# A hybrid decoder layer on one core: the gate and up projections as seven block products, with weight sums kept in DRAM

## The chip, the core and the metric

The kernel runs on one core of a Trainium2 chip. The metric is the device time of one execution in microseconds, as the median of several runs. Before the change it is 3034.36 us (three runs, 3031.14 to 3038.17).

## What is computed

One layer of a decoder for 2048 prompt tokens and 64 sample tokens (8 sequences of 8), together T = 2112. The first part (norm, a combined input projection, dilated window attention and a gated linear attention) is the same in both kernels. The change touches what follows:

```python
x1 = x + rmsnorm(concat(A, B) @ w_o, g_post)
h  = rmsnorm(x1, g_pre2)
gate = causal_dwconv3(h @ W_g)          # depthwise, 3 taps per channel
y  = x1 + rmsnorm((gelu(gate) * (h @ W_u)) @ W_down, g_post2)
```

The model width is 1024 (8 blocks of 128, KT), the hidden width 2816 (22 tiles of 128, NF). Everything is float32. The convolution's last two gate columns of every hidden channel are outputs too.

## The kernel before

Every product of matrices is made of three matmuls. `split` (L63 to L69) takes a float32 tile apart into a high part in a shorter format (`hi`, made by ScalarE, L66) and the rest (`lo` = source - `hi`, by GpSimd or VectorE, L69); `gemm` (L86 to L100) issues `wh·xh`, `wh·xl` and `wl·xh` for each block of the contraction and accumulates them in PSUM. `weight` (L73 to L84) loads a raw weight tile through SyncE's queue (L77) and splits it.

The span has three stages. Up to 1235 us run the first part's projections and the attention; this stage is not touched. Then comes `tail`, in two stages: the output projection (1235 to 1467 us) and the feed-forward part (1467 to 3011 us, with an end of 30 us behind it).

Tokens lie in the columns. The tail works in three chunks of 704 tokens (FCH: two halves of 352, 352 and 352, 448 and 256); a matmul works on one half.

- Output projection, `wo`, for each chunk: 8 output tiles (`pbo`), each of 8 blocks x 3 x 2 halves = 48 matmuls; the tile's weight (512 KB) is loaded and split anew in each chunk. VectorE copies the result out of PSUM (L61), ScalarE squares it (L1177) and the squares are added up (`bssq`, L1178) for the norm.
- `post`, for each chunk: a norm over the channels. Its matmuls `pn` (L125) sum the squares over the partitions; then come the gain (L1285), the addition of the residual (L1287), a second sum of squares, a second norm, and x1 and the factors of the second norm are stored in DRAM. It is a generator; its steps are interleaved with the next chunk's output tiles, and the last chunk's with the feed-forward part. `pb` (L136) spreads the factors over the partitions.
- `ffn_x`, for each chunk: x1 times the gain and the factor (L1309), then a split: the moving operand of the feed-forward part.
- `ffn`, for each chunk: hidden tiles in groups of 4, 4, 4, 4, 3 and 3 (FG). For each tile, a gate product (`pfg`, 48 matmuls, own weight of 512 KB), copies out of PSUM (L1339, L1340), two convolution taps on VectorE (L1349) with small copies of the two edge columns (`halo`, L1336 and L1347), the Gelu (L1355), an up product (`pfu`, 48 matmuls, another weight of 512 KB), the product of both (L1360) and its split (`hh`, `hl`). After a group, the down projection of its tiles (`pfd`) into 8 output tiles, added to an accumulator (L1390). All weights are loaded and split anew for each of the three chunks.
- `ffn_end` does the last group of the last chunk in two halves, and `final` makes the last norm, the residual (L1450 on VectorE, L1457 on GpSimd) and the store.

Tiles live in rings of buffers. The order of instructions on each engine is set by a scheduler of the framework, which goes by the order in the program, by its own model of durations and by when buffers come free; a dependency between two matmuls can pin their order. PSUM is used as four slots of two banks each.

Of the kernel before, what the change touches and what calls it, by code (L numbers as in the profile page):

```python
# [1 line left out]

# [24 lines left out]
FCH = ((0, 352, 352), (704, 352, 352), (1408, 448, 256))  # L27
FG = (4, 4, 4, 4, 3, 3)
# [6 lines left out]
class Layer:  # L35
# [35 lines left out]
    wc = None  # L71

    def weight(self, src, shape, lo_eng="p"):  # L73
        nc, p = self.nc, self.wpool
        pr, b = (self.xpool, self.wb[1] // 2) if self.wc is not None else (p, self.wb[1])
        raw = pr.tile(shape, F32, name=self.n("wr"), tag="wr", bufs=self.wb[0])
        nc.sync.dma_start(raw, src)  # L77
        if self.wc is not None:
            p = self.xpool if self.wc % self.wb[1] < b else p
            self.wc += 1  # L80
        hi = p.tile(shape, F32R, name=self.n("wh"), tag="wh", bufs=b)
        lo = p.tile(shape, F32R, name=self.n("wl"), tag="wl", bufs=b)
        self.split(hi, lo, raw, lo_eng)
        return hi, lo  # L84
# [30 lines left out]
    def rms_bcast(self, ssq, w, out, pool, psum, tag, shape=(128, 512), bufs=None, gap=2, lead=0, eng="a"):  # L115
# [8 lines left out]
        for j in range(nb):  # L124
            self.pnmm = nc.tensor.matmul(ps[:n, j:j + 1], ssq[:, o[j]:o[j] + n], self.ones, start=True, stop=True)  # L125
            self.gate("n", self.pnmm)
# [1029 lines left out]
    def subt(self, ps, c):  # L1156
        _, n0, n1 = FCH[c]
        return [(ps[:, 0, :n0], 0, n0), (ps[:, 1, :n1], n0, n1)]

    def t768(self, name, tag, bufs, dt=F32):  # L1160
        return self.npool.tile([128, self.W], dt, name=self.n(name), tag=tag, bufs=bufs)

    def hl(self, dt=F32R):
        p, b = (self.xpool, self.xb) if self.hc % 12 < self.xb // 2 else (self.npool, self.hlb - self.xb)
        self.hc += 1
        return tuple(p.tile([128, self.W], dt, name=self.n(n), tag="hl", bufs=b) for n in ("xh", "xl"))

    def raw(self):
        return self.xpool.tile([128, self.W], F32, name=self.n("br"), tag="raw", bufs=self.SB["xr"])

    def ssq_add(self, ssq, src, w, first, eng="p"):
# [3 lines left out]
        else:  # L1175
            sq = self.t768("sq", "sq", 2)
# [13 lines left out]

    def tail(self):
        tc, nc, a = self.tc, self.nc, self.a
        with ExitStack() as ctx:
            self.xpool = self.pool(ctx, "tx", side="right")
            self.gk = "h"
            self.W, self.hlb, self.wb = max(n0 + n1 for _, n0, n1 in FCH), self.SB["thl"], (2, 4)
            self.bx = [self.xpool.tile([128, self.W], F32, name=self.n("bx"), tag="px", bufs=3) for _ in range(3)]
            if self.SB["tw"]:
                self.wpool = self.pool(ctx, "tw")
            p = self.npool = self.pool(ctx, "tn")  # L1200
            if not self.SB["tw"]:
                self.wpool = self.pool(ctx, "tw")
            self.hc, self.xb = 0, self.SB["xb"]
            self.wc = 0 if self.SB["wx"] else None
            self.psum = self.pool(ctx, "tps", bass.MemoryType.PSUM)
            self.W, self.hlb, self.wb = max(n0 + n1 for _, n0, n1 in FCH), self.SB["thl"], (2, 4)
            pend = None
            for _ in self.wo_x(0):
                pass
            for c in range(3):  # L1210
                nxt = self.wo_x(c + 1) if c < 2 else self.ffn_x(0)
                for m, _ in enumerate(self.wo(c, self.xnext)):
                    if m >= 4:
                        next(nxt, None)
                    if pend is not None:
                        next(pend, None)
                        next(pend, None)
                for _ in nxt:
                    pass
# [476 lines left out]
```

## Time and profile before

| what | value |
|---|---|
| median of three runs | 3034.36 us |
| the profiled execution's own time | 3042.51 us |
| its span | 3040.7 us, mean granted TensorE clock 0.965 |
| first part | 0 to 1235 us |
| output projection | 1235 to 1467 us |
| feed-forward part | 1467 to 3011 us |
| last norm, residual, store | 3011 to 3041 us |
| bytes moved by the DMA | 378.92 MB, on average 125 GB/s |
| loads of gate and up weights | 132 of 512 KB |

The profile is one execution recorded by the hardware. Engines are PE (TensorE's matmuls), PEld (its weight loads), DVE (VectorE), ACT (ScalarE), POOL (GpSimd) and SP (SyncE, which here only issues transfers). A row of the groups of instructions has the line of the kernel, the engine, the operation, out<-in by the program's names with shapes and the count, then the busy time in us and the mean of one in ns, then the idle time of the engine right before them and what ended it. A row of the windows has, for a stretch of the span in us, its length, each engine's busy time with the number of instructions, the granted TensorE clock (1.00 is full), the share of time in which the DMA engines were busy and the GB/s they moved. A row of the waits has who waited for whom: us in total, times, the longest. A row of the timeline or of the chain has a start, a duration and the instruction; for a DMA the duration goes from issue to landing. Matmuls are pipelined, so what a matmul costs is the time from one start to the next and not its recorded duration.

### The profile page before, as it was taken

To read this page: it belongs to the slowest core of one execution; us is meant where nothing else is said; L and a number is where in the kernel's file an instruction comes from. 1 tells how busy PE (TensorE), PEld (TensorE's weight loads), DVE (VectorE), ACT (ScalarE), POOL (GpSimd) and SP (SyncE) were. 2 spreads that over 40 slices of the span, in tenths; PEclk is the share of its full clock that TensorE was granted. 3 is DMA by queue.
4 is the path that set the end of the run, shared out by engine and by line. 5 is a ranking of instruction groups with operands and counts; after the bars stand their busy time and mean duration, and the time that the engine had idled before them with its cause. 6 is when DMAs were issued, how large, how long until landed. Compare 5 with 4: busy or idle time off the path is not lost.

```text
span 3040.7 us, 50534 instructions
## 1 busy us (share of the span) xinstructions
PE 2870.4 (94%) x19738; PEld 2656.2 (87%) x19738; DVE 1382.0 (45%) x3263; ACT 1174.8 (39%) x2529; POOL 1426.2 (47%) x1014
## 2 busy tenths in 40 slices
PE   7988999999979999899899999999999999999996
PEld 5777788888767777798899999999999999999996
DVE  7686865344346655467732222371222236222225
ACT  5445444233256656333442232333222243322222
POOL 5656553334324465655443433574433366343343
PEclk9999999999989979999899999999999999999998
DMA  5323325699786665455432212252222224222222
GB/s 172 112 88 113 112 70 190 209 343 367 261 166 133 143 143 120 138 170 173 149 107 74 63 56 62 91 163 80 75 68 62 64 90 125 66 77 77 69 60 84
DMA packets 192975, 378.92 MB, mean 125 GB/s; under 512 B 19520, under 2 KB 91616, under 8 KB 187616
## 3 DMA queue, kind: packets, MB, share of 16 engines
q1 hardware_dynamic: 187680, 346.45, 36.2%
q0 software_dynamic: 5056, 29.24, 4.3%
q8 instruction: 155, 2.54, 0.4%
q14 instruction: 84, 0.69, 0.1%
HBM read 320.68 MB, written 54.94 MB: 124 GB/s over the span
## 4 chain that ended last, share of the span: by engine, by line
PE 51%; DVE 5%; ACT 1%; issue 1%; DMA 1%; POOL 0%; SPq 0%; ACTq 0%; DVEq 0%
PE pfd L94 16%; PE pfg L94 16%; PE pfu L94 15%; PE pbo L94 3%; DVE acc L1450 1%; DVE bssq L1178 1%; DVE bmo L1285 1%; DVE ct L1349 1%; DVE bmo L1287 0%; PE pn L125 0%; DMA br<-d_mixb 0%; ACT sq L1177 0%; DVE xl L69 0%; DVE br L1309 0%; DVE bmo L61 0%
## 5 line engine op out<-in xcount | busy, mean ns | idle before, releaser
L69 POOL TENSOR_TENSOR wl<-wr,wh 128x1024 fp32r<-128x1024 f32 (+2 forms) x386 | 780.2, 2025 | 1047.2 <-ACT wh L66 984.7
L66 ACT ACTIVATE wh<-wr 128x1024 fp32r<-128x1024 f32 (+2 forms) x389 | 347.7, 895 | 893.6 <-PE pfg L94 303.0
L1347 DVE COPY halo<-gt 128x2 f32<-128x2 f32 x66 | 48.8, 740 | 561.9 <-ACT gt L1339 561.9
L94 PE MATMUL pfu<-xh,wl 128*128 128x352 f32 (+2 forms) x1056 | 255.8, 323 | 0.0
L94 PE MATMUL pfg<-xh,wh 128*128 128x352 f32 (+2 forms) x1056 | 255.8, 323 | 0.0
L94 PE MATMUL pfu<-xh,wh 128*128 128x352 f32 (+2 forms) x1056 | 255.8, 323 | 0.0
L94 PE MATMUL pfu<-xl,wh 128*128 128x352 f32 (+2 forms) x1056 | 255.7, 323 | 0.0
L94 PE MATMUL pfg<-xh,wl 128*128 128x352 f32 (+2 forms) x1056 | 255.6, 323 | 0.0
L94 PE MATMUL pfg<-xl,wh 128*128 128x352 f32 (+2 forms) x1056 | 255.5, 323 | 0.0
L366 PE MATMUL pv<-wh,xh 128*128 128x256 f32 (+1 forms) x816 | 238.2, 292 | 9.0 <-DVE th L657 4.5
L94 PE MATMUL pfd<-hl,wh 128*128 128x352 f32 (+1 forms) x1008 | 243.3, 324 | 1.5 <-POOL hl L69 1.5
L94 PE MATMUL pfd<-hh,wh 128*128 128x352 f32 (+1 forms) x1008 | 240.1, 325 | 3.6 <-ACT hh L66 3.6
L94 PE MATMUL pfd<-hh,wl 128*128 128x352 f32 (+1 forms) x1008 | 242.9, 324 | 0.0
L366 PE MATMUL pv<-wl,xh 128*128 128x256 f32 (+1 forms) x816 | 235.2, 288 | 0.0
L366 PE MATMUL pv<-wh,xl 128*128 128x256 f32 (+1 forms) x816 | 234.8, 288 | 0.0
L1390 DVE TENSOR_TENSOR acc<-acc,pfd 128x352 f32<-128x352 f32 (+1 forms) x224 | 105.0, 517 | 282.3 <-PE pfd L94 282.3
L1511 ACT ACTIVATE ass<-ass,aml 128x256 f32<-128x256 f32 (+1 forms) x384 | 174.5, 456 | 122.3 <-DVE aml L1506 120.4
L94 PE MATMUL pq<-xh,wh 128*128 128x512 f32 (+2 forms) x480 | 173.3, 368 | 11.1 <-ACT xh L223 8.1
L94 PEld LDWEIGHTS pfu<-xh,wl 128*128 128x128 f32 x1056 | 176.8, 188 | 2.6
L94 PEld LDWEIGHTS pfg<-xh,wl 128*128 128x128 f32 x1056 | 176.8, 188 | 2.5
L94 PEld LDWEIGHTS pfg<-xh,wh 128*128 128x128 f32 x1056 | 176.7, 188 | 2.5
L94 PEld LDWEIGHTS pfg<-xl,wh 128*128 128x128 f32 x1056 | 176.6, 188 | 2.5
(316 smaller groups left out, 6540.0 us busy)
## 6 DMA issues: line engine op xcount, KB each, us to landing
wr<-in_wu SPq DMA_DIRECT2D x132, 512.0 KB
wr<-in_wt SPq DMA_DIRECT2D x95, 512.0 KB
wr<-in_wd SPq DMA_DIRECT2D x96, 256.0 KB
skp<-in_ckt SPq DMA_DIRECT2D x16, 1024.0 KB
svp<-in_cv SPq DMA_DIRECT2D x16, 1024.0 KB
av<-out_o_vp SPq DMA_DIRECT2D x192, 64.0 KB
wr<-in_wo SPq DMA_DIRECT2D x24, 512.0 KB
raw<-in_xn SPq DMA_DIRECT2D x40, 256.0 KB
```

Source lines behind the costliest of these rows:

```text
L66: nc.scalar.activation(hi, src, AF.Copy)
L69: (nc.gpsimd if lo_eng == "p" else nc.vector).tensor_tensor(lo, src, hi.bitcast(F32), op=ALU.subtract)
L94: mm = nc.tensor.matmul(o, ww[:, k, :], xx[:, s0:s0 + n], start=(k == order[0] and i == 0), stop=(k == order[-1] and i == 2))
L366: mm = nc.tensor.matmul(ps[:m, :256], x[:, t0:t0 + m], w[:, k % 4, :], start=(k == 0 and i == 0), stop=(k == KT - 1 and i == 2))
L1178: return (nc.gpsimd if eng == "p" else nc.vector).tensor_tensor(ssq[:, :w], ssq[:, :w], sq[:, :w], op=ALU.add)
L1285: nc.vector.scalar_tensor_tensor(o[:, :w], o[:, :w], self.gv[:, 1, m:m + 1], rb[:, :w], op0=ALU.mult, op1=ALU.mult)
L1347: nc.vector.tensor_copy(halo[:, f, :], gt[:, npr:npr + 2])
L1349: nc.vector.scalar_tensor_tensor(ct[:, :npr], gt[:, tap:tap + npr], self.cw[:, f, tap:tap + 1], ct[:, :npr], op0=ALU.mult, op1=ALU.add)
L1390: nc.vector.tensor_tensor(acc[m][:, s0:s0 + n], acc[m][:, s0:s0 + n], pz, op=ALU.add)
L1450: st = e1.scalar_tensor_tensor(am, am, self.gv[:, 3, m:m + 1], rb[:, :w], op0=ALU.mult, op1=ALU.mult)
L1511: nc.scalar.activation(ssb[:, sc:sc + nk], ssb[:, sc:sc + nk], AF.Exp, bias=self.ml[:, idx, h:h + 1], scale=-1.0, accum_out=self.ml[:, idx ...
```

## The change

**Chunks.** Four chunks of 528 tokens (two halves of 264), hidden groups of 2, 4, 4, 4, 4, 4 tiles. All buffers of the tail have 528 columns. PSUM is used as eight single banks.

**Gate and up projection.** `strassen` replaces `gemm` there. It takes two hidden tiles together as a block matrix: two halves of the contraction (4 blocks each) by two tiles, times two halves of the contraction by two halves of the tokens. In place of eight block products there are seven, of 4 blocks x 3 matmuls x 264 columns, so 84 matmuls a call where the plain way has 96; a call is made for each pair of tiles and each of gate and up, 88 calls in all. Four PSUM banks (`pfa`, `pfb`, `pfd`, `pfe`) take the products, three of them twice, the second product added onto the first. ScalarE copies bank `pfa` out twice (`p1`, `u2`), VectorE makes five additions out of PSUM (L1379 of the new kernel).

**Sums of weights and tokens.** The products need sums of the blocks of both operands. The weights' sums are made in the first chunk: `wsrc` loads the two raw tiles (two buffers, `wraw`, L1174 of the new kernel), makes four sums of 128x512 on VectorE, splits seven blocks (the high part on ScalarE, the rest on GpSimd four times and VectorE three times, in turn) and stores each split block (512 KB) in a new DRAM scratch `wst` (L1372). The next three chunks load these blocks, seven for each call, into a ring of 8 slots. The down weights are handled in the same way (`down_w`, scratch `wdst`, L1407) and use the same ring and the same two raw buffers. The tokens' sums are made in `ffn_x` for each chunk: 16 differences of 264 columns beside the 8 gains, on VectorE, and 14 splits (8 of the low parts on GpSimd, 6 on VectorE), into a ring of 28 slots, which is exactly what one chunk needs.

**Order.** The down projection of a group is now a generator that runs after the gate call of the next group. The token sums of the next chunk are interleaved with the last group's down projection.

**Output projection.** Each of the eight weights is loaded and split once, in the first chunk, and kept on chip. ScalarE copies the results out of PSUM. The `post` steps stand in a queue, two steps for each output tile; their norm matmuls `pn` are pinned behind the matmul that was issued last (`pin`). The last chunk's post step and the end of the one before run in the first two groups of the feed-forward part.

```diff
-FCH = ((0, 352, 352), (704, 352, 352), (1408, 448, 256))
-FG = (4, 4, 4, 4, 3, 3)
+H = 264
+FCH = tuple((2 * H * c, H, H) for c in range(4))
+FG = (2, 4, 4, 4, 4, 4)
...
             self.pnmm = nc.tensor.matmul(ps[:n, j:j + 1], ssq[:, o[j]:o[j] + n], self.ones, start=True, stop=True)
+            if pin:
+                self.after(self.pnmm, self.lastmm)
...
+    def wsrc(self, c, f, z):
+        nc, a = self.nc, self.a
+        wt = a["wst"][f // 2, z]
+        if c:
+            for i in range(7):
+                t = self.slot("w", [128, 2, 512], F32R, "ws")
+                nc.sync.dma_start(t.bitcast(F32), wt[i])
+                yield t.rearrange("p a (k c) -> p a k c", k=4)
+            return
+        g0, g1 = (self.wraw(a["wu"][2 * (f + j) + z]) for j in range(2))
+        t3 = self.spool.tile([128, 3, 4, 128], F32, name=self.n("wt"), tag="wt", bufs=1)
+        lo, hi = slice(0, 4), slice(4, 8)
+        nc.vector.tensor_tensor(t3[:, 0], g0[:, lo], g1[:, lo], op=ALU.subtract)
+        nc.vector.tensor_tensor(g1[:, lo], g1[:, lo], g1[:, hi], op=ALU.add)
+        nc.vector.tensor_tensor(t3[:, 1], g1[:, lo], g0[:, lo], op=ALU.subtract)
+        nc.vector.tensor_tensor(t3[:, 2], g0[:, hi], t3[:, 1], op=ALU.subtract)
+        for i, src in enumerate((g0[:, lo], g0[:, hi], t3[:, 1], g1[:, lo], t3[:, 0], t3[:, 2], g1[:, hi])):
+            t = self.slot("w", [128, 2, 512], F32R, "ws")
+            t4 = t.rearrange("p a (k c) -> p a k c", k=4)
+            self.split(t4[:, 0], t4[:, 1], src, "pvpvpvp"[i])
+            yield t4
+            nc.sync.dma_start(wt[i], t.bitcast(F32))
...
+        for i, (bank, new, ev) in enumerate((
+                (pa, True, lambda: nc.scalar.copy(p1, pa[:, :H])),
+                (pb, True, lambda: add(o11, p1, pb)),
+                (pa, False, lambda: nc.scalar.copy(u2, pa[:, :H])),
+                (pe, True, lambda: add(u4, u2, pe)),
+                (pd, True, lambda: add(o22, u4, pd)),
+                (pe, False, lambda: add(o12, u2, pe)),
+                (pd, False, lambda: add(o21, u2, pd)))):
+            w = next(ws)
+            for k in range(4):
+                xh, xl = xs[self.PROD[i]][k]
+                for j, (ww, xx) in enumerate(((0, xh), (0, xl), (1, xh))):
+                    self.lastmm = nc.tensor.matmul(bank[:, :H], w[:, ww, k, :], xx, start=new and k == 0 and j == 0,
+                                                   stop=k == 3 and j == 2, skip_group_check=not new)
+            ev()
...
+            if c == 0:
+                raw = self.wraw(a["wo"][m])
+                hi, lo = (self.slot("w", [128, 8, 128], F32R, n) for n in ("wh", "wl"))
+                self.split(hi, lo, raw, self.SB["we"][m])
+                self.wow.append((hi, lo))
...
+        xs = self.xnext = {n: [None] * 4 for n in ("b11", "t1", "b21", "b22", "t2", "t3", "t4")}
...
+    PROD = ("b11", "b21", "t2", "t1", "t3", "b22", "t4")
```

How the order moves, at the places of which the prediction speaks. The rows of the new kernel have the new kernel's line numbers.

First TensorE, in the output projection, at the second norm of a chunk's post step: `pbo` are output tiles, `pn` the norm's matmuls. Before:

```order
L94 MATMUL pbo_15076<-xl_14597,wh_15072 128x352 x2
L94 MATMUL pbo_15076<-xh_14596,wl_15073 128x352 x2
L125 MATMUL pn_15139<-c_ones,bssq_2552_14755 128x1 x6
L94 MATMUL pbo_15166<-xh_14371,wh_15162 128x352 x2
L94 MATMUL pbo_15166<-xl_14372,wh_15162 128x352 x2
```

And after:

```order
L90 MATMUL pbo_15112<-xh_14606,wl_14523 128x264
L90 MATMUL pbo_15113<-xh_14606,wl_14523 128x264
L121 MATMUL pn_15174<-c_ones,bssq_2556_14753 128x1 x5
L90 MATMUL pbo_15219<-xh_14948,wh_14072 128x264
L90 MATMUL pbo_15220<-xh_14948,wh_14072 128x264
```

The matmuls around it are the same kind of work. In the new kernel the first norm of a post step stands one output tile (48 matmuls) into the next chunk, and the second, shown here, seven tiles (336 matmuls) behind the first.

Next SyncE's queue of transfers in the first chunk of the feed-forward part: `wr` are raw weights. Before:

```order
L77 DMA wr_17233<-in_wu 128x1024
L77 DMA wr_17299<-in_wu 128x1024
L77 DMA wr_17360<-in_wd 128x512
L77 DMA wr_17393<-in_wd 128x512
L77 DMA wr_17426<-in_wd 128x512
```

And after, where `d_wst` is the scratch of split weight sums and `ws` a slot of the ring:

```order
L1407 DMA d_wdst<-ws_18114 128x1024
L1174 DMA wr_18171<-in_wu 128x1024
L1372 DMA d_wst<-ws_18195 128x1024
L1372 DMA d_wst<-ws_18178 128x1024
L1372 DMA d_wst<-ws_18246 128x1024
L1372 DMA d_wst<-ws_18229 128x1024
L1372 DMA d_wst<-ws_18280 128x1024
L1174 DMA wr_18318<-in_wu 128x1024
L1174 DMA wr_18320<-in_wu 128x1024
```

The raw loads, which stood one behind the other, now stand behind stores that wait for the splits of their blocks.

Last VectorE, early in the feed-forward part, where a post step meets the hidden tiles: `bmo` are the output projection's results, `ct` and `gt` a hidden tile's gate. Before:

```order
L112 SCALAR_TENSOR_TENSOR rcy_16008<-rcz_16009,rcy_16008 128x6
L1347 COPY halo<-gt_16021 128x2
L1349 SCALAR_TENSOR_TENSOR ct_16022<-gt_16021,c_cw,ct_16022 128x704 x2
L1336 COPY gt_16331<-halo 128x2
L1360 TENSOR_TENSOR ct_16022<-ct_16022,pfu_16038 128x352 x2
L1285 SCALAR_TENSOR_TENSOR bmo_15322<-bmo_15322,c_gvec,brb_15999 128x704
```

And after, where `u` and `gt` on the left are sums of block products out of PSUM:

```order
L1379 TENSOR_TENSOR u_2872_16864<-u_2871_16863,pfe_16861 128x264
L1379 TENSOR_TENSOR gt_16855<-u_2872_16864,pfd_16860 128x264
L1458 COPY halo<-gt_16855 128x2
L1302 SCALAR_TENSOR_TENSOR bmo_15872<-bmo_15872,c_gvec,brb_16833 128x528
L1302 SCALAR_TENSOR_TENSOR bmo_15946<-bmo_15946,c_gvec,brb_16833 128x528
L1302 SCALAR_TENSOR_TENSOR bmo_16012<-bmo_16012,c_gvec,brb_16833 128x528
L1302 SCALAR_TENSOR_TENSOR bmo_16089<-bmo_16089,c_gvec,brb_16833 128x528
```

Gains of the post step now stand between two additions out of PSUM of the same call, the next of which (`gt` of the other tile) follows nine rows further on.

More of the change, by code (lines that the diff above doesn't have):

```diff
@@ L1 @@
 from contextlib import ExitStack
+from itertools import chain
 import numpy as np
@@ new lines, in ffn @@
+            if not (last and c == 3):
+                down = self.down(c, gi, f - G, G, hs, acc, last)
+        if c == 3:
+            nc.sync.dma_start(a["o_cp"], halo)
+            nc.sync.dma_start(a["o_cs"], self.co)
+            return self.ffn_end(c, acc, hs, f - G, G)
+        nxt = self.ffn_x(c + 1)
+        for _ in down:
+            next(nxt, None)
+        for _ in nxt:
+            pass
+        return self.final(c, acc, self.fssq, 0, w)
+    def ffn_end(self, c, acc, hs, f0, G):
+        nc, a = self.nc, self.a
+        wds = [self.down_w(c, len(FG) - 1, m, f0, G) for m in range(KT)]
+        t0 = FCH[c][0]
```

388 lines of the change are left out of this document (207 added, 181 removed).

## Prediction

> **What bounds the kernel now.** I read the page's head and its chain first, then the busy times by stage, then the cadence of the matmuls, and last the single operations from which the new work can be priced.
>
> ```profile
> span 3040.7 us, 50534 instructions
> PE 2870.4 (94%) x19738; PEld 2656.2 (87%) x19738; DVE 1382.0 (45%) x3263; ACT 1174.8 (39%) x2529; POOL 1426.2 (47%) x1014
> PE 51%; DVE 5%; ACT 1%; issue 1%; DMA 1%; POOL 0%; SPq 0%; ACTq 0%; DVEq 0%
> ```
>
> TensorE is busy for 94% of the span, the others for less than half. The chain that ended last lies on TensorE for 51%, hardly anywhere else. The windows by stage say where this holds (attention and all before it end at 1235, the output projection at 1467, the feed-forward part at 3011):
>
> ```profile
> core 0: us, PE busy (x) PEld busy (x) DVE busy (x) ACT busy (x) POOL busy (x), PEclk, DMA share, GB/s
> 1235.00:1467.00 232.00, 204.01 (x1232) 199.32 (x1230) 136.99 (x175) 77.52 (x99) 129.46 (x61) 0.92 0.48 159
> 1360.00:1380.00 20.00, 10.25 (x50) 9.95 (x49) 12.91 (x23) 8.44 (x11) 9.91 (x6) 0.66 0.41 133
> 1467.00:3011.00 1544.00, 1538.69 (x9561) 1514.01 (x9560) 501.16 (x868) 502.48 (x787) 679.87 (x382) 1.00 0.27 83
> 1600.00:1800.00 200.00, 200.00 (x1243) 200.00 (x1242) 47.73 (x86) 58.62 (x88) 76.67 (x43) 1.00 0.22 67
> ```
>
> In the feed-forward stage TensorE is busy for 1538.69 of 1544 us at a granted clock of 1.00: only fewer or shorter matmuls help there, and VectorE (501 us) and the DMA (share 0.27) have room. In the output projection it is busy for 204 of 232 us; inside, at 1360 to 1380, for half the time at a clock of 0.66.
>
> **Term 1, the matmuls.** One of 352 columns takes 200/1243 = 160.9 ns from start to start. For 256 columns I take the last group, where sixteen steps lie between these two rows of the timeline:
>
> ```profile
> 3004.08 0.29 PE L94 MATMUL pfd<-hl,xh 128*128 128x256 f32 x1
> 3005.99 0.28 PE L94 MATMUL pfd<-hh,xl 128*128 128x256 f32 x1
> ```
>
> That is 1.91/16 = 119.4 ns. A matmul of 264 columns is not in the trace; in proportion to 352 it takes 120.7 ns, on the line through both points 122.9, and I take 122. Before there are 6336 matmuls in gate and up, 3168 in down, 1152 in the output projection, 352 columns on average: 10656 x 160.9 = 1715 us. After, gate and up are 11 pairs x 2 x 4 chunks = 88 calls of 7 products x 4 blocks x 3 = 84, so 7392; down has 4224, the output projection 1536: 13152 x 122 = 1605 us. **-110**, between -127 and -98. The seven products alone would give an eighth of gate and up, 127; down gains nothing.
>
> **Term 2, the output projection.**
>
> ```profile
> PE pn L125 <- DVE bssq L1178: 20.7, 2, 11.0
> PE pbo L94 <- ACT xh L66: 5.4, 1, 5.4
> 1323.89 2.92 DMA wr<-in_wo
> ```
>
> Two norm matmuls stand in TensorE's order ahead of the next chunk's matmuls and wait 20.7 us for VectorE. After, they stand behind the next chunk's first output tile and seven tiles further on, so that about 48 and 336 matmuls are queued ahead of them; only if VectorE is still later than that does the next chunk stand behind the pinned one again. The PSUM copies move to ScalarE, which is busy for 77.5 of 232 us; 16 of 24 weight loads with their splits go. **-20**, between 0 (the wait returns with four chunks) and -28 (the 5.4 us and the rest go too).
>
> **Term 3, the old feed-forward stage's own loss**, 1544 less 9504 x 0.1609 = 1529: **-15**, replaced by terms 4 to 6.
>
> **Term 4, the first two groups of the first pass.** Their TensorE work is 6 calls of 84 and 96 down matmuls, 600 x 0.122 = 73 us. What VectorE has to do in this time is priced from these groups:
>
> ```profile
> L1349 DVE SCALAR_TENSOR_TENSOR ct<-gt,c_cw,ct 128x704 f32<-128x704 f32 x88 | 92.3, 1048 | 10.5 <-ACT ct L1340 9.1
> L1285 DVE SCALAR_TENSOR_TENSOR bmo<-bmo,c_gvec,brb 128x704 f32<-128x704 f32 x24 | 34.8, 1519 | 1.2 <-ACT brb L59 1.2
> L1390 DVE TENSOR_TENSOR acc<-acc,pfd 128x256 f32<-128x256 f32 x32 | 13.3, 414 | 0.0
> L1347 DVE COPY halo<-gt 128x2 f32<-128x2 f32 x66 | 48.8, 740 | 561.9 <-ACT gt L1339 561.9
> L1336 DVE COPY gt<-halo 128x2 f32<-128x2 f32 x64 | 12.7, 199 | 1.4
> L69 DVE TENSOR_TENSOR xl<-br,xh 128x704 fp32r<-128x704 f32 x23 | 31.4, 1367 | 27.0 <-ACT xh L66 27.0
> ```
>
> No weight sum stands in the trace. In proportion to its columns, one of 512 lies between 0.76 (L1349) and 1.10 us (L1285); I take 0.85, nearer to the row that has 88 of its kind amid the same work, and 0.90 for 528 columns. Six calls have 6 x (4 sums + 3 splits) = 42 of 512: 35.7 us; 30 additions out of PSUM at 0.42: 12.6; taps and products, 18 of 528: 16.2; 12 small copies (740 and 199 ns): 5.6; the last chunk's post step, which falls here now, 23 of 528 at 1.07: 24.6; the first token sums, 8 gains at 1.09, 16 differences of 264 at 0.48 and 6 splits at 1.03: 22.6. Together 117 us, against 73. Some of it lies beside the end of the output projection: **+40**, between 10 (much of the post step and the token sums is done by then, at the low prices) and 65 (at the high ones, and a raw load of 2.92 us bare at the start, since most slots of the token sums come free with the output projection's last tile). TensorE waits here, for weights and for tokens.
>
> **Term 5, groups three to six of the first pass.** TensorE: 4 calls and 192 down matmuls, 4 x 10.25 + 23.4 = 64.4 us. VectorE: 28 of 512, 12 of 528, 36 additions out of PSUM and 8 copies, 23.8 + 10.8 + 15.1 + 3.8 = 53.5. For GpSimd, ScalarE and the DMA there are these rows:
>
> ```profile
> L69 POOL TENSOR_TENSOR wl<-wr,wh 128x512 fp32r<-128x512 f32 x96 | 124.5, 1302 | 304.0 <-ACT wh L66 290.4 <-PE pb L136 7.6 <-issue 6.0
> L66 ACT ACTIVATE wh<-wr 128x512 fp32r<-128x512 f32 x96 | 60.6, 631 | 265.1 <-PE pfg L94 100.0 <-PE pfd L94 82.7 <-PE pfu L94 44.3
> ```
>
> ```profile
> 600.00:800.00 200.00, 199.18 (x1734) 158.04 (x1736) 89.72 (x174) 72.24 (x90) 81.96 (x37) 1.00 0.93 342
> 700.00:730.00 30.00, 30.00 (x249) 23.02 (x247) 9.27 (x22) 10.25 (x13) 9.97 (x4) 1.00 1.04 399
> ```
>
> A call moves two loads and seven stores of 0.524 MB, 4.72 MB, a down tile 0.79; a group 4 x 4.72 + 8 x 0.79 = 25.2 MB. At 399 GB/s that is 63 us, just inside 64.4. The chain of one call matters more: raw load 2.92, three sums 2.6, then GpSimd's splits of the third, fifth and seventh product, 0.6 + 3 x 1.3 = 4.5, and only then are both raw buffers free: 10.0 us against 10.25, with nothing queued. But SP's queue holds the next raw loads behind stores that wait for these splits, and VectorE, 83% busy, has the sums behind other work; I take 12.4 us a call (the 2.4 are my choice: two to three VectorE operations of waiting) and 3 us for the down tiles, which use the same two raw buffers. 4 x 2.2 + 3 = 12 a group, **+48**, between 16 (a third: the 8-slot ring bridges the rest) and 80 (20 a group).
>
> By the Trainium skill, "DMA: Bandwidth & Descriptors", section "Where 436 GB/s comes from", transfers between HBM and SBUF are bound at about 358 GB/s for a core. That would be an estimate of 70.4 us for a group, 6 above TensorE's 64.4, and changes the sum only if it came on top of the chain: 24 us more. The row of 30 us with 399 GB/s disagrees.
>
> **Term 6, the later three passes.** No sums, no splits: 3.67 MB of weights for each 10.25 us, 358 GB/s, covered at 399; at 342 a call takes 10.73, 0.5 more, which the down tiles' spare (0.524 MB in 2.93 us) and the ring give back. Before, a weight of 0.5 MB served 48 matmuls, 7.7 us; now seven serve 84, so the cover is thin. Inside a call a product that writes the bank of the last but one waits for that bank's copy: 1.46 us of cover, against 0.42 and whatever VectorE has queued. And at three chunk borders the new token sums (22.6 us of VectorE) can't start before the old ones are read, since the ring holds just one chunk's: down of the last group, 23.4 us, is the cover. I take 6 us a border and 0.15 us for each of 66 calls: **+28**, between 10 and 70 (1 us a call).
>
> Where GpSimd's additions and the end of the kernel lie, nothing moves: the last half chunk has 264 columns for 256.
>
> **Sum.** 3040.7 - 110 - 20 - 15 + 40 + 48 + 28 = 3011.7 us of span. The profiled execution's own time was 3042.51, 1.8 above its span and 0.27% above the median of the runs shown, 3034.36. So 3013.5 x 0.9973 = **3005 us**, 1% faster. Combined, the terms' ends reach 50 us down and 60 up: the forecast's own range is 2955 to 3065.
>
> **The rivals.** *A, the cover holds:* terms 4 to 6 come to 46 instead of 116, because the ring runs ahead and the sums fit beside the matmuls. For it speaks VectorE's 48 of 200 us in the window 1600 to 1800, against it that term 4's 117 us fit into no 73. 3011.7 - 70, at the median's scale 2936 us.
>
> *B, slower: VectorE becomes the bound of the first pass, because its operations stretch beside GpSimd.* Place: the calls in which GpSimd splits weights while VectorE forms sums. These rows show how long they can get:
>
> ```profile
> L1450 DVE SCALAR_TENSOR_TENSOR acc<-acc,c_gvec,frb 128x704 f32<-128x704 f32 x16 | 32.9, 2116 | 0.0
> L1457 POOL TENSOR_TENSOR acc<-fx,acc 128x704 f32<-128x704 f32 x16 | 36.5, 2303 | 2.2 <-DVE acc L1450 2.2
> ```
>
> The same kind and size that takes 1048 ns at L1349 takes 2116 where GpSimd's additions run beside it, and a copy of two columns takes 740 at L1347 but 199 at L1336. At 2116 (1.54 for 512 columns, 1.59 for 528) a group's VectorE work is 81 us, 17 above TensorE, 67 in all for term 5's 48; term 4's 117 become 183, +110 for +40. 3011.7 + 19 + 70, at the median's scale 3094. It decides the sign from some 1.59 us for 704 columns (my prices come to 1.27 in term 4). Against it: at L1349 GpSimd works 44% of the time too, and in a group now 31 us of splits of weights and some 5 of hidden units in 64. The Trainium skill, "SBUF — State Buffer", section "Who interferes with whom", says that VectorE's second port pair is GpSimd's and an exclusive lock; by that rule two-input sums and splits exclude each other, and B follows. The two rows of this case agree in direction.
>
> *C, slower: the DMA sustains less.* The window of 200 us moved only 342 GB/s at a share of 0.93. At that rate a group's 25.2 MB take 73.7 us, +9.3 each, on top of the chain: +37; and if the ring bridges nothing, 66 calls x 0.48 = +32 later. 3074. Against it, 399 over 30 us.
>
> *D, the change does not do what it says:* a matmul of 264 columns costs 135 ns or more, 13 x 13152 = +171: 3176. The 119.4 ns for 256 speak against it.
>
> **How the numbers follow.** Forecast 0.55, A 0.19, B 0.10, C 0.10, D 0.03, no net change 0.03. About 0.2%, 6 us, is what a measurement of this kernel can tell. Of the forecast's own range 0.43 lies faster than that, 0.04 within, 0.08 slower. Faster: 0.43 + 0.19 = 0.62; same 0.04 + 0.03 = 0.07; slower 0.08 + 0.23 = 0.31. The range reaches from just below A to just above C, 2925 to 3080; B's full price, D and the lowest of A stay out.
>
> **What would show it.** Right: matmuls of 264 start every 121 to 123 ns; no wait of the norm matmuls above 3 us in the output projection; the first pass takes 73 + 4 x 64.4 = 331 us of matmuls and some 88 more, with DMA near 380 GB/s; each later pass (11 pairs, 5 or 6 groups of down) some 350 us, TensorE over 95% busy. Wrong: a first pass above 450 us, with VectorE over 90% busy and its 512-column sums above 1.2 us (B), or with a DMA share of 1 at 342 GB/s or less (C); later passes with TensorE below 93%, waiting for weight slots or for PSUM copies behind VectorE.

## The result: 3118.87 us, 2.8% slower

The changed kernel takes 3118.87 us (median of four runs, 3115.91 to 3120.58) against 3033.23 us for the kernel before; the ratio is 1.0279 with a 95% interval of 1.0261 to 1.0297. The prediction was 3005 us, with a range from 2925 to 3080.

The page of the changed kernel:

```profile
span 3114.1 us, 57988 instructions
PE 2821.7 (91%) x22255; PEld 2605.2 (84%) x22255; DVE 1735.3 (56%) x4085; ACT 1125.8 (36%) x2633; POOL 1148.7 (37%) x926
```

TensorE is busy for 49 us less than before, and the span is 73 us longer: it now waits. The windows by stage say where (output projection; the first seven calls of the first pass; its next three groups; two stretches of a later pass's length, each of which begins some 20 to 25 us behind the first matmul of the second and of the third pass; last, 30 us inside a later pass):

```profile
core 0: us, PE busy (x) PEld busy (x) DVE busy (x) ACT busy (x) POOL busy (x), PEclk, DMA share, GB/s
1235.00:1442.00 207.00, 196.93 (x1610) 196.41 (x1611) 96.96 (x149) 85.02 (x170) 92.40 (x54) 0.97 0.43 144
1442.00:1635.00 193.00, 140.35 (x926) 131.25 (x925) 148.94 (x231) 78.70 (x150) 83.22 (x58) 0.81 0.72 260
1635.00:1907.00 272.00, 219.78 (x1588) 207.33 (x1587) 176.08 (x253) 96.40 (x168) 123.35 (x84) 0.95 0.77 276
2015.00:2381.00 366.00, 358.83 (x2920) 357.16 (x2918) 173.53 (x349) 81.76 (x150) 67.37 (x45) 1.00 0.85 303
2381.00:2748.00 367.00, 359.95 (x2920) 357.97 (x2918) 172.98 (x359) 82.05 (x150) 67.31 (x45) 0.99 0.85 301
2050.00:2080.00 30.00, 30.00 (x248) 30.00 (x247) 12.22 (x26) 7.36 (x14) 5.53 (x4) 1.00 1.02 407
```

The later passes run nearly as hoped: the second and the third take 370 and 367 us from first matmul to first matmul, with TensorE full. The first pass, 548 us from 1442 to 1990, does not: neither VectorE (65% in the third row) nor the DMA (0.77) nor GpSimd (45%) is full there, so no single engine's work is the bound. The waits of the third row's stretch name who is late:

```profile
PE pfe L1392 <- ACT ws L68: 15.0, 10, 3.6
PE pfe L1392 <- DVE ws L71: 13.8, 9, 2.4
PE pfe L1392 <- DVE u L1379: 7.5, 8, 0.9
```

TensorE waits for the split weight blocks (`ws`), above all for those of the fourth product (the first use of bank `pfe`), which needs the second of the four sums. One call can be followed through the timeline: the raw loads in SyncE's queue, the first use of a raw tile on ScalarE, the first sum on VectorE.

```profile
1639.38 2.00 SPq L1174 DMA_DIRECT2D wr<-in_wu  x2
...
1653.43 0.33 SPq L1174 DMA_DIRECT2D wr<-in_wu  x1
...
1658.24 0.46 SPq L1174 DMA_DIRECT2D wr<-in_wu  x1
```

```profile
1646.43 1.15 ACT L68 ACTIVATE ws<-wr 128x512 fp32r<-128x512 f32 x2 [6.00 <-issue]
```

```profile
1648.88 0.68 DVE L1363 TENSOR_TENSOR wt<-wr,wr 128x512 f32<-128x512 f32 x1
...
1668.11 1.42 DVE L1363 TENSOR_TENSOR wt<-wr,wr 128x512 f32<-128x512 f32 x1
```

Issued from 1639.4, used at 1646.4; the next call's second raw tile is issued only at 1658.2, and its first sum comes 19.2 us after this call's. For the 84 matmuls of a call TensorE needs 10.25 us at 122 ns each.

### The profile page after: what moved, and what is told of

Its sections match the earlier page's. It is cut to its first block, busy times and chain, and to the rows that moved or that the text cites. A ratio compares the mean times of both kernels' runs of the same rounds, so it can differ in the third digit from the quotient of the medians.

```text
span 3114.1 us, 57988 instructions
## 1 busy us (share of the span) xinstructions
PE 2821.7 (91%) x22255; PEld 2605.2 (84%) x22255; DVE 1735.3 (56%) x4085; ACT 1125.8 (36%) x2633; POOL 1148.7 (37%) x926
## 5 line engine op out<-in xcount | busy, mean ns | idle before, releaser
L90 PE MATMUL pfd<-hh,ws 128*128 128x264 f32 x2816 | 479.9, 288 | 36.4 <-ACT ws L68 9.4
L90 PEld LDWEIGHTS pfd<-hh,ws 128*128 128x128 f32 x2816 | 402.3, 191 | 42.1 <-ACT hh L68 11.5
L1392 PE MATMUL pfe<-xh,ws 128*128 128x264 f32 x1408 | 304.1, 295 | 59.2 <-ACT ws L68 25.0
L71 POOL TENSOR_TENSOR wl<-wr,wh 128x1024 fp32r<-128x1024 f32 x102 | 253.9, 2496 | 209.4 <-ACT wh L68 170.6
L1392 PE MATMUL pfa<-xh,ws 128*128 128x264 f32 x1408 | 303.7, 295 | 14.3 <-ACT ws L68 5.3
L1392 PEld LDWEIGHTS pfe<-xh,ws 128*128 128x128 f32 x1408 | 239.7, 195 | 69.3 <-ACT ws L68 28.3
L90 PE MATMUL pfd<-hl,ws 128*128 128x264 f32 x1408 | 296.8, 287 | 0.2 <-POOL hl L71 0.2
L1392 PE MATMUL pfd<-xh,ws 128*128 128x264 f32 x1408 | 292.0, 288 | 2.2 <-ACT xh L68 1.4
L1392 PEld LDWEIGHTS pfa<-xh,ws 128*128 128x128 f32 x1408 | 239.8, 196 | 21.6 <-ACT ws L68 6.7
L1392 PEld LDWEIGHTS pfd<-xh,ws 128*128 128x128 f32 x1408 | 234.9, 192 | 3.0 <-ACT xh L68 1.7
L1609 ACT ACTIVATE ass<-ass,aml 128x256 f32<-128x256 f32 (+1 forms) x384 | 174.5, 456 | 119.1 <-DVE aml L1604 116.7
L71 POOL TENSOR_TENSOR ws<-wr,ws 128x512 fp32r<-128x512 f32 (+1 forms) x92 | 128.3, 1396 | 206.2 <-ACT ws L68 163.0
```

Of the source, the lines that this page charges most:

```text
L71: (nc.gpsimd if lo_eng == "p" else nc.vector).tensor_tensor(lo, src, hi.bitcast(F32), op=ALU.subtract)
L90: mm = nc.tensor.matmul(o, ww[:, k, :], xx[:, s0:s0 + n], start=(k == order[0] and i == 0), stop=(k == order[-1] and i == 2))
L1392: self.lastmm = nc.tensor.matmul(bank[:, :H], w[:, ww, k, :], xx, start=new and k == 0 and j == 0, stop=k == 3 and j == 2, skip_group_chec ...
L1609: nc.scalar.activation(ssb[:, sc:sc + nk], ssb[:, sc:sc + nk], AF.Exp, bias=self.ml[:, idx, h:h + 1], scale=-1.0, accum_out=self.ml[:, idx ...
```

## The experiments

**Theory 1**: a loop sets the first pass. A raw load, the sums, the splits and the release of the two raw buffers follow one another, with no second call in flight. **Theory 2**: VectorE and GpSimd slow each other and are the bound. **Theory 3**: the DMA's rate is the bound.

The attention's end, which no kernel here changes, lies between 1222 and 1236 us in these traces. The later passes, which only nostore, load0, dwraw and all4 touch, spread over 1101 to 1115 us in the other changed versions. A single total is therefore read to 7 us at best, and what counts is this table from the traces (us). Kernels for which the text gives no ratio ran once. The time is the median where a kernel ran several times, and the stages are those of the profiled run. The gap is from the attention's last matmul to the first of the output projection; "start" goes to the begin of the eighth call and has 107 us of matmuls (7 calls, 288 down matmuls); "rest" is the rest of the first pass, 247 us of matmuls; "later" goes to the last matmul of the kernel, 1063 us of matmuls. In the changed kernel 40 of the first pass's down matmuls, 5 us, fall behind the rest's end, so that its rest loses 5 us more than the columns say and its later passes 5 us less.

| kernel | time | gap | output proj. | start | rest | later |
|---|---|---|---|---|---|---|
| before | 3033.2 | 0 | 231 | | | |
| changed | 3118.9 | 17.0 | 198.6 | 192.7 | 355.3 | 1103.5 |
| nostore | 3031.8 | 16.4 | 198.3 | 177.1 | 287.1 | 1100.7 |
| raw4 | 3039.0 | 16.4 | 198.7 | 171.9 | 290.1 | 1106.8 |
| nosum | 3089.3 | 16.7 | 198.1 | 176.2 | 348.2 | 1100.6 |
| load0 | 2980.3 | 16.5 | 198.1 | 164.5 | 249.4 | 1098.9 |
| actld | 3118.7 | 15.1 | 199.7 | 191.0 | 358.9 | 1100.7 |
| raw4ld | 3043.5 | 16.0 | 199.2 | 175.4 | 287.9 | 1110.8 |
| raw4st | 3059.0 | 17.0 | 198.2 | 176.2 | 302.8 | 1108.7 |
| raw4dve | 3031.4 | 17.1 | 198.2 | 173.1 | 273.4 | 1114.6 |
| dwraw | 3026.9 | 16.9 | 197.5 | 174.5 | 257.5 | 1126.5 |
| post3 | 3042.1 | 17.1 | 223.5 | 163.0 | 272.3 | 1114.5 |
| all4 | 3037.2 | 19.2 | 222.9 | 159.2 | 254.4 | 1131.6 |
| woq | 3010.0 | 18.4 | 198.4 | 172.2 | 272.4 | 1104.9 |
| leftq | 3024.5 | 19.7 | 201.5 | 172.8 | 274.3 | 1104.7 |
| left | 3028.6 | 18.8 | 199.4 | 171.5 | 273.4 | 1108.7 |
| leftqp | 3024.0 | 20.0 | 199.5 | 177.4 | 273.2 | 1105.7 |
| addrq | 3022.0 | 18.3 | 199.4 | 172.7 | 272.4 | 1109.1 |
| addr | 3023.8 | 16.1 | 198.8 | 172.2 | 274.5 | 1111.2 |

### Buffers, stores, sums, or all of the preparation

**nostore**, nearly all stores of the first pass gone (those of the down weights too, in lines not shown here):

```diff
-            nc.sync.dma_start(wt[i], t.bitcast(F32))
+            if f == 0 and z == 0:
+                nc.sync.dma_start(wt[i], t.bitcast(F32))
...
```

> Leaves out: the first pass stores only the blocks of its first call and of the first two groups' down weights, 7 + 16 of 202 stores; the later passes load these same blocks again and again, so their bytes and counts stay. Theory 1 (the loop raw load, sums, splits, store, next raw load, through one queue with two raw buffers, sets the first pass): the raw loads no longer stand behind stores, a first-pass group falls from 90 us to 70 to 75, the run by 80 to 130 us to 2990 to 3040. Theory 2 (VectorE and GpSimd slow each other and are the bound): the splits and sums stay, the run falls by less than 30 us. Theory 3 (the DMA's rate, 276 GB/s at a share of 0.77, is the bound): 3.67 of 4.72 MB of a call are gone, a fall of 100 us or more, as in theory 1.

Measured: 3031.8 us, 87 less; the rest of the pass falls by 68 us. Theory 2 alone can't do that. Rows of the chain of waits say what the stores had done to the raw loads, first in the changed kernel (4.9 to 6.5 us in the four that show a whole load), then without the stores (3.2 to 4.2 us in seven):

```profile
1857.43 6.51 DMA wr<-in_wu
...
1903.88 4.97 DMA wr<-in_wu
```

```profile
1778.54 3.20 DMA wr<-in_wu
```

**raw4**, four raw buffers:

```diff
-name=self.n("wr"), tag="wr", bufs=2)
+name=self.n("wr"), tag="wr", bufs=4)
```

> Four raw weight buffers for two, nothing else. Theory 1: the next call's raw loads can be issued a call ahead, a group falls from 90 us to about 76, the run by 50 to 100 us, to 3020 to 3070; if the stores' waits in SyncE's queue hold the loads and not the buffers, it falls by less than 30. Theory 2: no change, within 15 us of 3119. Theory 3: no change either, since the same bytes are moved.

Measured: 3039.0 us, 80 less, ratio to the kernel before 0.999 (0.9975 to 1.0005). All bytes and all operations are still there, and theories 2 and 3 expected no change, so both fall as the main cause: theory 1 holds. (The framework's scheduler may order instructions anew with four buffers; that was not looked at.) A loop can be shortened (no stores) or overlapped with itself (more buffers); both give the same 287 to 290 us.

**nosum**, the sums left out:

```diff
-        nc.vector.tensor_tensor(t3[:, 0], g0[:, lo], g1[:, lo], op=ALU.subtract)
...
-g0[:, lo], g0[:, hi], t3[:, 1], g1[:, lo], t3[:, 0], t3[:, 2], g1[:, hi]
+g0[:, lo], g0[:, hi], g0[:, lo], g1[:, lo], g0[:, hi], g1[:, lo], g1[:, hi]
```

> Leaves out: the four weight sums of each first-pass call; blocks of the raw weights are split in their places, so that loads, splits, stores and matmuls stay. Theory 1: the chain of a call gets shorter by the third sum's wait, some 3 us of 16, the run falls by 40 to 70 us. Theory 2: VectorE loses 4 of its 7 long operations in a call, some 4.7 us of 16 and the same again in GpSimd's waits, the run falls by 80 us or more. Theory 3: no change.

Measured: 3089.3 us, 30 less, of which only 7 in the rest of the pass. Both theories had expected more (40 to 70, and 80 or more), so the sums by themselves are a small part of the loop.

**load0**, prepared blocks loaded in the first pass too:

```diff
-        if c:
+        if c or f or z:
             for i in range(7):
...
```

> Leaves out: all preparation of weights in the first pass but for the first call and the first two groups' down weights; the other calls load seven prepared blocks (the first call's) as the later passes do. This prices the whole preparation: if it alone makes the first pass long, that pass takes about 366 us as the later ones do, plus the first call's bare chain and the last chunk's post step (some 40 us), 405 for 561: the run at 2945 to 2970. If the first pass stays above 450 us, something else than the weights (the post step, the token sums) holds it.

Measured: 2980.3 us, 10 above the expected range, with a first pass of 414 us for 405. The rest of the pass takes 249.4 us, two above its matmuls, so the preparation explains that stretch. The start still takes 164.5 us, 58 above its matmuls. The first call, whose weights are still prepared here, takes 40 us of it, and in its first 29.8 us VectorE, with token sums, weight sums and the post step, is nearly full:

```profile
1445.70:1475.50 29.80, 12.85 (x39) 8.46 (x37) 26.17 (x36) 11.36 (x20) 13.01 (x9) 0.56 0.60 196
```

In the 125 us behind this call VectorE is busy for 72: something else holds them.

### The queue, or GpSimd

**actld**, the raw loads from ScalarE's queue, with two buffers:

```diff
-        self.nc.sync.dma_start(raw[:, :nk]
+        self.nc.scalar.dma_start(raw[:, :nk]
```

> Two raw buffers as in the changed kernel, but the raw weights' loads are issued from ScalarE's queue, so that no store stands ahead of them in SyncE's. If the order in the one queue holds the raw loads (the half of theory 1 that blames the queue), the run falls by 50 us or more, towards the 3039 of four buffers; if the two buffers do (each load must wait until the call before has split its last block), it falls by less than 25 us.

Measured: 3118.7 us, no change. The half of theory 1 that blamed the order in SyncE's queue falls: the buffers hold the loads. (The loads now stand behind ScalarE's own splits and copies, a new wait that this run does not part off; raw4, where the loads stay in SyncE's queue, does not have it.)

**raw4ld**, the same with four buffers:

> Four raw buffers and the raw loads in ScalarE's queue. A first-pass group was 75 us with four buffers, 73 with hardly any stores, 64.4 would be TensorE alone. If the stores' waits in SyncE's queue are what is left, 3 us a group and as much at the start: 3020 to 3030. If VectorE and GpSimd are left, no change from 3039 within 8 us.

Measured: 3043.5 us (ratio to before 1.0019, 1.0007 to 1.003), no gain. **raw4st**, the stores from ScalarE's queue, `nc.scalar.dma_start(wt[i], ...)`:

> Four raw buffers, and the stores of the split blocks issued from ScalarE's queue, where each waits for its split by GpSimd or VectorE and holds ScalarE's own splits and PSUM copies behind it. If the queue order is what is left: 3020 to 3030. If ScalarE's new waits outweigh it: 3045 to 3080.

Measured: 3059.0 us, with a rest 13 us longer than raw4's: in it ScalarE waits 43 us for GpSimd's splits.

**raw4dve**, four buffers and all low parts of the weight blocks on VectorE:

```diff
-self.split(t4[:, 0], t4[:, 1], src, "pvpvpvp"[i])
+self.split(t4[:, 0], t4[:, 1], src, "vvvvvvv"[i])
```

> Four raw buffers, and in the first pass VectorE makes all seven low parts of a call (GpSimd keeps the down weights, the hidden units and the tokens). If VectorE's operations are long because GpSimd's splits run beside them (0.68 us alone, 1.1 on average in the changed kernel), the sums fall to 0.75 us on average, VectorE stays at about its 76%, and a group falls from 75 to 70 us: 3010 to 3025. If not, VectorE has 4 x 4 x 1.1 = 18 us more in a group and becomes the bound: a group of 85 us, 3075 to 3090.

Measured: 3031.4 us, short of the gain that was expected, but the rest is 17 us shorter than raw4's though VectorE got four more operations a call. The group of the third sum in these stretches (mean ns behind the busy time), in the changed kernel, with four buffers, and with GpSimd off the blocks:

```profile
L1365 DVE TENSOR_TENSOR wt<-wr,wr 128x512 f32<-128x512 f32 x12 | 16.1, 1344 | 0.2
```

```profile
L1365 DVE TENSOR_TENSOR wt<-wr,wr 128x512 f32<-128x512 f32 x14 | 13.7, 977 | 0.5
```

```profile
L1365 DVE TENSOR_TENSOR wt<-wr,wr 128x512 f32<-128x512 f32 x13 | 9.0, 689 | 0.1
```

The third sum takes 689 ns on average where GpSimd splits no block beside it and 1344 ns where it does; over all four sums these averages are 0.75 and 1.18 us. Theory 2's mechanism is real, but it lengthens the loop; it is not the bound.

### What is left of the first pass

**dwraw**, on raw4dve: the down weights are split anew in every pass and not stored (the `if c:` branch and the store of `down_w` go).

> On the version with four raw buffers and VectorE's low parts: the down weights are loaded raw and split anew in every pass, as in the kernel before, and not stored: 8 x 0.52 of 25.2 MB of a first-pass group are gone. If the DMA (share 0.92, 347 GB/s) is what holds a group at 71 us: 66 to 67 us a group, 3010 to 3018. If it is the chain of sums, splits and raw buffers: no change in the first pass, and up to 10 us more in the later ones, where GpSimd splits beside VectorE: 3028 to 3042.

Measured: the rest falls by 16 us, the later passes grow by 12, the total is 4.5 less. The windows of the rest (1630 to 1900 in raw4dve, 1620 to 1878 in dwraw):

```profile
1630.00:1900.00 270.00, 248.41 (x1970) 243.86 (x1968) 205.54 (x367) 118.44 (x214) 89.73 (x59) 0.99 0.92 347
```

```profile
1620.00:1878.00 258.00, 251.24 (x2035) 250.39 (x2034) 221.05 (x383) 127.32 (x223) 93.35 (x59) 0.99 0.85 310
```

Once the loop is overlapped, the stores do count: without those of the down weights TensorE is busy for 97% instead of 92%. Whether it is their bytes or the ring slots that they hold, this run does not part.

**post3**, on raw4dve: three post steps for each output tile.

```diff
-                        for _ in range(2):
+                        for _ in range(3):
                             if posts and next(posts[0], self) is self:
```

> On the version with four raw buffers and VectorE's low parts: three steps of the post queue for each output tile, not two, so that the post step of the third chunk is done in the output projection, where VectorE has room, and only the last one falls into the feed-forward part. If VectorE's queue sets the first calls (the first takes 43 us for 10): 8 to 15 us less, 3016 to 3024. If the token sums wait for their slots, which come free with the last output tile: no change.

Measured: 3042.1 us. The start is 10 us shorter, the output projection 25 us longer: the norms' matmuls wait there now, for 15 us by the trace. **all4**, these two with raw4dve and the next edit:

> Four raw buffers, VectorE's low parts, raw down weights, three post steps for each tile and the output projection's first loads in ScalarE's queue. If the three single changes add up at the middle of their expectations: 3031 - 13 - 17 - 11 = 2990, faster than the kernel before by 1.5%. If only the contention-free ones count: 3010 to 3030.

Measured: 3037.2 us, ratio 1.0 (0.9981 to 1.002): post3's loss and dwraw's later passes eat the gain.

### The gap ahead of the output projection

In the changed kernel the loads of the first blocks and weights stand in SyncE's queue behind the attention's last four stores; before, a part stood ahead. **woq**, on raw4dve:

```diff
-                nc.sync.dma_start(r, a["mixb"][:, k - 4, t0:t0 + w])
+                (nc.sync if c else nc.scalar).dma_start(r, a["mixb"][:, k - 4, t0:t0 + w])
...
+                raw = self.wraw(a["wo"][m], q=nc.scalar if m < 4 else None)
```

> On the version with four raw buffers and VectorE's low parts (3031 us): the loads of the first chunk's four mixb blocks and of the first four output-projection weights are issued from ScalarE's queue. In the changed kernel they stand in SyncE's queue behind the attention's last four stores, which wait for their data, and the first output matmul starts 17 us after the attention's last one; in the kernel before, six of these loads stood ahead of those stores and there was no gap. If the queue's order is the cause: a gap of 5 us or less, 3017 to 3022. If the buffers come free only when the attention ends: the gap stays at 14 us or more, no change.

Measured: the gap stays, 18.4 us. (The total, 3010 us, is low because the attention ended 11 us earlier and the later passes were 10 us shorter than in raw4dve; no stage that the edit touches gained.) Here the loads were early, and the split waited, with the wait put down to the attention's last store (ScalarE's timeline):

```profile
1217.90 7.92 ACTq L1260 DMA_DIRECT2D br<-d_mixb  x2
1232.45 0.64 ACT L68 ACTIVATE xh<-br 128x528 fp32r<-128x528 f32 x1 [13.98 <-DMA d_mixa<-amo]
```

I took the first token slot to lie on the addresses of the tile that this store reads; no view here shows addresses. **leftq** (on woq), **left** (loads in SyncE's queue again) and **leftqp** (leftq with the last post step's additions on GpSimd) reorder the slots:

```diff
+                hl = self.slots["hl"]
+                self.slots["hl"] = hl[8:16] + hl[:8] + hl[16:]
```

> Four raw buffers, VectorE's low parts, the output projection's first loads in ScalarE's queue, and its first four moving blocks in slots whose addresses the attention frees before its merge (the last four, which wait for the merge's stores anyway, take the others). If the address is what the first split waits for, the gap between the attention's last matmul and the first output matmul falls from 18 us to 6 or less: 12 us less than without, 3000 to 3020. If the gap stays above 14 us, the address is not the cause either.

> The same slots, but with the loads in SyncE's queue, where they stand behind the attention's last stores. If queue and address each suffice to hold the first matmul, the gap stays at 14 to 17 us, as it did when only the queue was changed; if the address alone is the cause, it falls to 6 us or less.

> As leftq, and the last chunk's post step makes its 8 residual additions and 7 additions of squares on GpSimd, 11 to 15 us off VectorE in the first calls of the feed-forward part. If VectorE's load is what the first calls wait for, the first two groups get 8 to 15 us shorter; if GpSimd's additions stretch VectorE's operations in turn, no gain, or up to 10 us longer.

Measured: gaps of 19.7, 18.8 and 20.0 us. With the new order the loads themselves were issued late (in leftq from 1238.7); that the raw token buffer now lay on that tile is again not shown. leftqp's start is 5 us longer. leftq takes 3024.5 us, ratio 0.9959 (0.9945 to 0.9972). **addrq** and **addr** lay two slots there that are needed last:

```diff
+                self.slots["hl"] = hl[:2]
+                self.hl()
...
+                self.scnt["hl"] = 0
```

> As leftq, with two slots that are needed last laid on the addresses of the attention's last output tile, so that neither a first slot nor a raw buffer lies there. If the address is the cause, loads and splits of the first four blocks are done beside the attention's merge and the gap falls from 20 us to 3 to 8 us: 12 to 16 us less, 3008 to 3013. If it stays above 14 us, I have no cause for it.

> The same addresses, loads in SyncE's queue behind the attention's last stores. If the queue alone suffices to hold them: a gap of 12 us or more. If not: 3 to 8 us as in addrq.

Measured: gaps of 18.3 and 16.1 us. So the address, if it was a cause, was not the only one. In addrq the third and fourth load still wait, and ScalarE's order has a split of a late block ahead of the first weight's:

```profile
1235.83 0.64 ACT L68 ACTIVATE xh<-br 128x528 fp32r<-128x528 f32 x1 [7.04 <-DMA d_mixa<-amo]
...
1246.94 1.71 ACT L68 ACTIVATE xh<-br 128x528 fp32r<-128x528 f32 x3 [6.60 <-DMA bx<-in_xn]
1248.55 1.04 ACT L68 ACTIVATE wh<-wr 128x1024 fp32r<-128x1024 f32 x1
```

What sets the gap stays open. addrq takes 3021.96 us, ratio 0.9947 (0.9931 to 0.9964), the best of the versions that were timed several times. Four raw buffers, GpSimd off the weight blocks and the moved loads and slots together make the change 0.5% faster than the kernel before; four buffers alone made it even (0.999). Since the gap did not fall, the parts of the last step are not shown.

## Why the prediction was wrong

By its own terms, with TensorE's matmuls as the base:

- **Term 1 held.** 248 matmuls start in 30 us, 121 ns each, against 122.
- **Term 2 held in sum.** The norms' waits are gone, and the output projection takes 198.6 us from its first matmul to its last. The gap of 17 us ahead of it, which no term had, takes half of the gain back: 231.4 us before, 215.6 after, -16, where terms 1 and 2 together gave -18. That the sum fits is luck: the stage gained 33 us, and the gap that no term had lost 17.
- **Term 4 was half.** In the start (one call and one group's down projection more than the term has), TensorE takes 193 - 107 = 86 us more than its matmuls, not 40. With nearly all weights prepared (load0), 58 of them are left. Some 30 of these lie in the first call, at whose begin VectorE is busy for 26 of 30 us: there the term's reason, VectorE's time, fits. In the other 125 us VectorE is busy for 58%, so those 28 us are not VectorE's time added up, and what they wait for, one behind the other, was not settled; moving post work forward (post3) shortened the start by 10 us.
- **Term 5 is the step that failed, by the size of its chain.** "I take 12.4 us a call", with 48 us for four groups and 80 as the upper end: the rest of the pass takes 355 - 247 = 108 us more than its matmuls. That the chain from a raw load to the release of its buffer is a call's time was right: raw4 shows it. Its length was not. In the trace the eight calls of the rest that stand whole and without down matmuls between them take 15.7 to 17.2 us, 16.5 on average, from a call's first matmul to the next one's. One turn of the loop, in SyncE's queue, on ScalarE and on VectorE:

```profile
1731.98 1.76 SPq L1174 DMA_DIRECT2D wr<-in_wu  x2
...
1749.25 2.01 SPq L1174 DMA_DIRECT2D wr<-in_wu  x2
```

```profile
1738.03 1.15 ACT L68 ACTIVATE ws<-wr 128x512 fp32r<-128x512 f32 x2 [2.56 <-DMA wr<-in_wu]
```

```profile
1740.53 1.81 DVE L1363 TENSOR_TENSOR wt<-wr,wr 128x512 f32<-128x512 f32 x1
...
1742.60 0.68 DVE L1364 TENSOR_TENSOR wr<-wr 128x512 f32<-128x512 f32 x1
...
1744.90 1.77 DVE L1365 TENSOR_TENSOR wt<-wr,wr 128x512 f32<-128x512 f32 x1
...
1748.30 1.77 DVE L1366 TENSOR_TENSOR wt<-wr,wt 128x512 f32<-128x512 f32 x1
```

From one pair of raw loads to the next 17.3 us pass. The load, priced at 2.92 us from a quiet stretch, is used after 6.0. The first sum starts 2.5 us later, behind other work of VectorE. The four sums, priced at 0.85 us each between two rows, take 6.0 us in all, and stand among so much other work of VectorE that 9.5 us pass from the first one's start to the last one's end. The term had 10.0 us "with nothing queued" and 2.4 for all queues. How the excess parts among these links over the whole pass was not measured: leaving the sums out gave back only 7 us.
- **What no term had: a slow clock behind the waits.** A wait was priced at its own length. In the rest of the changed kernel's first pass 245 of some 1990 matmuls start 0.15 to 0.27 us apart, most of them 0.22; at 122 ns each they would take 24 us less, an estimate from their starts. By the same count it is 15 us in the start. One such stretch, behind a wait of 2 us, has a granted clock of 0.50 (a row of the timeline, then one of the windows):

```profile
1821.32 0.51 PE L1392 MATMUL pfe<-xh,ws 128*128 128x264 f32 x2 [1.96 <-DVE ws L71]
```

```profile
1821.80:1825.10 3.30, 3.30 (x18) 3.30 (x17) 2.18 (x3) 0.63 (x1) 0.60 (x1) 0.50 0.94 324
```

- **Term 6 was close.** The later passes take 1103.5 - 1063 = 40 us more than their matmuls, not 28. Terms 4 and 5, with 46 and 60 us too little, are nearly the whole miss of 114.
- **The rivals.** A fell with terms 4 and 5, D with term 1. B had the right place and a real mechanism but the wrong consequence: VectorE's operations do stretch, the third sum to twice its length, and VectorE is still only 65% busy. C fell for the changed kernel: 407 GB/s for 30 us in a later pass, and 276 GB/s at a share of 0.77 in the first pass. In raw4dve, at 347 GB/s and a share of 0.92, the rate is near that of C's own row (342 at 0.93), and there fewer stores did help. Of the signs of being wrong, the long first pass came (548 us, above 450), but with neither a full VectorE nor a full DMA beside it: the case that no rival had. The figure of some 358 GB/s that the Trainium skill gives for a core ("DMA: Bandwidth & Descriptors", "Where 436 GB/s comes from") is exceeded by the row of 407 GB/s. The Trainium skill's rule on the port that VectorE and GpSimd share ("SBUF — State Buffer", "Who interferes with whom") agrees in direction with 689 against 1344 ns.

The weights' preparation, without the first call's and the first two groups' down weights, costs 28 + 106 us of the changed kernel (changed against load0). Two more buffers give back 86 of these 134; GpSimd off the blocks 17 in the rest of the pass, less 1 in the start.

## What to carry to other kernels

Where work that was prepared elsewhere is now made on the way, write its chain as a loop: from the release of its input buffers round to the next release. If one set of buffers carries it, the chain's length is the period, however idle each engine looks. Here a second set was worth 80 us, another queue nothing, and leaving the sums out 30. Price each link from rows of the crowded stage that it will run in, not from a quiet one, and look at the granted clock behind the waits that are left.

## What was not expected of the hardware

- A sum of 128x512 on VectorE took 0.75 us on average with GpSimd off the weight blocks and 1.18 us beside its splits; the third of the four 0.69 and 1.34 us.
- A load of 512 KB took 3.2 to 4.2 us in the first pass without stores and 4.9 to 6.5 us with them.
- The DMA moved 407 GB/s over 30 us (2050 to 2080) while TensorE was full.
- Shortly behind a wait, TensorE's matmuls of 264 columns started 0.22 us apart for some 3 us (1821.8 to 1825.1, granted clock 0.50), then 0.12 us again.
